# A diffusion block on one core: the state space's parameters at the head of the program, the modulation's early pieces behind the state-space stage

## The chip, the cores and the metric

One core of one Trainium2 chip runs the whole program. The metric is the device time of one execution in microseconds; a kernel's figure is the median over its runs. Times from the profile are microseconds from the first instruction of one profiled execution.

## The reference, cut to what matters

The reference is one layer of a hybrid backbone over 1024 latent tokens and 256 context tokens, 1024 features wide, all in float32.

```python
mod_x = silu(c) @ w_mod + b_mod              # six vectors: shift1, scale1, gate1, shift2, scale2, gate2
mod_c = silu(c_ctx) @ w_mod + b_mod
px = modulate(rmsnorm(x, g_norm_mix), sh1, sc1) @ w_in      # x: 1024 tokens
pc = modulate(rmsnorm(ctx, g_norm_mix), ch1, cc1) @ w_in    # context: 256 tokens
conv_x, fnet_x, qkv_x, ssm_x = split_cols(px)
y_conv = conformer_conv(conv_x, ...)         # gate, 31 taps, layernorm, silu, 256x256
y_fnet = fourier_mix(fnet_x, ...)
y_na   = neighbourhood_attention(q, k, v, k_ctx, v_ctx, rpb)
y_ssm  = s5_bidirectional(ssm_x, ssm_c, a_re, a_im, log_dt, b, c, d, w_glu, ...)
out = group_rmsnorm(concat(...)) @ w_out + b_out
x_mid = x + gt1 * out
x = x_mid + gt2 * mlp(modulate(rmsnorm(x_mid), sh2, sc2))   # squared ReLU, 4096 wide
return rmsnorm(x, g_final)
```

The state space runs in both directions over the context and then over the latent tokens, with 16 groups of 16 channels and 64 states. Its parameters come from `log_dt`, `a_re` and `a_im` through an exponential, a sine and a cosine, and powers of the result up to the ninth.

## The kernel before, in words

Data lies with features on the 128 partitions and tokens along the free axis. Latent tokens are worked on in two halves of 512 (`hf`). The products with `w_in` are done by tiles of 128 output features; each float32 operand is split into a high and a low part, so that a tile takes three matmuls for each of eight feature chunks.

The stages that the change touches, in program order:

- The **head**, lines 308 to 327. It loads x, and for each of eight chunks k the modulation weights for shift1 and scale1 (`load_wm`, two pieces of 512 KB), runs a small product with the conditioning vectors (`gemv`), sets `gsc`, and norms chunk k of both halves (`norm_x`: `nt` on VectorE, the high part on ScalarE, the low part `xl` on VectorE). Three weight tiles of `w_in` (12 and 13 for the state space, 8 for the keys) are loaded and split, with the low part `wlo` on GpSimd.
- The **x tiles** for these three, both halves (line 403 and on), 24 matmuls each, all recorded at line 364.
- **`mods(n)`**, line 335: n steps of the rest of the modulation. The first 16 of 32 pieces (gate1 and shift2) are done here, each a load of 512 KB (`wmB`, line 340), sixteen small matmuls (line 344), an eviction, and a pair of matmuls of the piece before (line 349). After each eight pieces VectorE sets `mod` (line 351). The other 16 are done in the attention.
- The **context**: eight loads (line 401), sum of squares, norm, and the context's part of tiles 12, 13 and 8. The results for the state space go to a tensor in memory, `us_d`.
- The state space's **parameters**, lines 440 to 581: about 60 small GpSimd operations, some 40 on VectorE, two sines on ScalarE, and the loads of `log_dt`, `bnat` and `cnat`.
- The **state-space blocks**: eight blocks of two groups. `ssm_setup(b)` builds the block's matrices on GpSimd and VectorE (`ca`, line 624, is the last GpSimd operation of it), with matmuls `pk` and transposes; `ssm_tables(b)` makes sine and cosine tables; `ssm_main(b)` reads `us_d` into `U`, multiplies, rotates (`ro`, from line 692), scans and writes `ys_d`. Setup and tables are called one block ahead.
- Then the tiles of `w_in` 9, 4 and 5, the values (`w_v`), `conv_in(0)` (two tiles whose product is `cv`, line 787), the GLU of the state space, the Fourier mixing, `conv_in(1)`, the queries, and the taps of the convolution on VectorE (line 1020). The attention follows, with an order of TensorE written by hand.

Up to the attention the order on each engine is not the program's: a planner takes, at each step of a modelled time, the ready operation that stands first in the program, and so fixes one in-order queue for each engine and for SP, which issues the loads. `tc.issue_after(ins)` makes what a block issues on the engine of `ins` stand behind `ins` in that queue. Tiles come from rings by tag: `wraw`, with three buffers, holds half of each `wm` pair, every `wmB` piece and every raw tile of `w_in` and `w_v`.

Of the kernel before, what the change touches and what calls it, by code (L numbers as in the profile page):

```python
# [8 lines left out]
F32 = mybir.dt.float32  # L9
# [8 lines left out]
P = 128  # L18
# [31 lines left out]
def body(tc, A, out, dbg=None):  # L50
# [256 lines left out]

    load_x(0)
    SP.dma_start(ident, A["cst"][:, 0:P])
    for k in range(8):  # L310
# [88 lines left out]
    for k in range(8):  # L399
        ctt.append(xp.tile([P, TC], F32, name="ctt", tag="hc", bufs=16))  # L400
        SP.dma_start(ctt[k], A["ctxT"][:, k, :])
# [8 lines left out]
    mods(4)  # L410
# [22 lines left out]
    mods(5)  # L433

    sset = ExitStack()
    sp = open_pool("ssm", "right", stack=sset)
    tst = ExitStack()
    tp = open_pool("tiny", "right", stack=tst)

    def tn(name, pool=None):  # L440
        return (pool or tp).tile([P, 16], F32, name="t_" + name)

    E_ = G
    ldt = tn("ldt")
    for d in range(2):
        SP.dma_start(ldt[d * 64:(d + 1) * 64, :], ap(A["log_dt"], d * 16, [[0, 64], [1, 16]]))

    def expparts(x, pre):

        n, r, w, sc = tn(pre + "n"), tn(pre + "r"), tn(pre + "w"), tn(pre + "s")  # L450
        E_.tensor_scalar(n, x, 1.4426950408889634, MAGIC, ALU.mult, ALU.add)
        E_.tensor_scalar(n, n, MAGIC, 1.0, ALU.subtract, ALU.mult)
        E_.tensor_scalar(n, n, -126.0, 127.0, ALU.max, ALU.min)
        V.scalar_tensor_tensor(r, n, -0.693145751953125, x, ALU.mult, ALU.add)
        V.scalar_tensor_tensor(r, n, -1.42860682030941723e-6, r, ALU.mult, ALU.add)
        E_.tensor_scalar(w, r, 1.0 / 5040, 1.0, ALU.mult, ALU.mult)
        for c in (1 / 720, 1 / 120, 1 / 24, 1 / 6, 0.5, 1.0):
            V.scalar_tensor_tensor(w, w, c, r, ALU.add, ALU.mult)
        E_.tensor_scalar(n, n, 127.0, 8388608.0, ALU.add, ALU.mult)
        ni = tp.tile([P, 16], I32, name="t_" + pre + "i")  # L460
        V.tensor_copy(ni, n)
        V.tensor_copy(sc, ni.bitcast(F32))
        return sc, w

    def tt(o, a, b, op, eng=None):
        (eng or E_).tensor_tensor(o, a, b, op)
        return o

    are, aim = C("are", 0, 16), C("aim", 0, 16)
    sc, w = expparts(ldt, "d")  # L470
    dt = tn("dt")
    tt(dt, sc, w, ALU.mult)
    tt(dt, dt, sc, ALU.add)
    ar, tau = tn("ar"), tn("tau")
    tt(ar, are, dt, ALU.mult)
    tt(tau, aim, dt, ALU.mult)
    E_.tensor_scalar(tau, tau, 0.15915494309189535, 1.0, ALU.mult, ALU.mult)
    kk = tn("kk")

    def frac(x):  # L480
        E_.tensor_scalar(kk, x, MAGIC, MAGIC, ALU.add, ALU.subtract)
        tt(x, x, kk, ALU.subtract)

    frac(tau)
    sc, w = expparts(ar, "e")
    Em, Ee = tn("Em"), tn("Ee")
    tt(Em, sc, w, ALU.mult)
    tt(Ee, Em, sc, ALU.add)
    V.scalar_tensor_tensor(Em, sc, -1.0, Em, ALU.add, ALU.add)
    sn, s2, cm = tn("sn"), tn("s2"), tn("cm")  # L490
    S.activation(sn, tau, AF.Sin, scale=TWO_PI)
    S.activation(s2, tau, AF.Sin, scale=PI_)
    tt(cm, s2, s2, ALU.mult)
    E_.tensor_scalar(cm, cm, -2.0, 1.0, ALU.mult, ALU.mult)
    pw_r = tp.tile([P, 10, 16], F32, name="pw_r")
    pw_i = tp.tile([P, 10, 16], F32, name="pw_i")
    V.memset(pw_r[:, 0, :], 1.0)
    V.memset(pw_i[:, 0, :], 0.0)
    mr, mi = tn("mr"), tn("mi")
    tt(pw_i[:, 1, :], Ee, sn, ALU.mult)  # L500
    V.scalar_tensor_tensor(pw_r[:, 1, :], cm, 1.0, Ee, ALU.add, ALU.mult)
    V.scalar_tensor_tensor(mr, cm, 1.0, Em, ALU.add, ALU.mult)
    tt(mr, mr, cm, ALU.add)
    mi = pw_i[:, 1, :]
    zr, zi, iv, t0 = tn("zr"), tn("zi"), tn("iv"), tn("t0")
    tt(iv, are, are, ALU.mult)
    tt(t0, aim, aim, ALU.mult)
    tt(iv, iv, t0, ALU.add)
    V.reciprocal(iv, iv)
    tt(zr, mr, are, ALU.mult)  # L510
    tt(t0, mi, aim, ALU.mult)
    tt(zr, zr, t0, ALU.add)
    tt(zr, zr, iv, ALU.mult)
    tt(zi, mi, are, ALU.mult)
    tt(t0, mr, aim, ALU.mult)
    tt(zi, zi, t0, ALU.subtract)
    tt(zi, zi, iv, ALU.mult)

    def cmul(orr, oi, ar_, ai_, br_, bi_, shape, tg, eng, neg_i=False):

        def tmp_():
            if shape is None:
                return sp.tile([P, 2, 160], F32, name="cm", tag="ss", bufs=4).rearrange(
                    "p a b -> p (a b)")[:, :256].rearrange("p (a b) -> p a b", a=16)
            return tp.tile(shape, F32, name="cm", tag=tg, bufs=2)
# [43 lines left out]
    for i in range(2):  # L569
        SP.dma_start(bn[i], A["bnat"][:, i, :])  # L570
# [12 lines left out]
    GB = 2  # L583
# [1355 lines left out]
```

## Time and profile before

| | us |
|---|---|
| median of 3 runs | 1326.41 |
| lowest and highest run | 1323.22, 1332.71 |
| the profiled execution | 1320.52 |
| its span, first to last instruction | 1318.4 |
| TensorE busy | 1182.3 |
| VectorE busy | 1025.8 |
| GpSimd busy | 799.6 |
| ScalarE busy | 650.7 |

The busy times are sums over the whole span, and the stages have different limits. PE is TensorE's matmuls, PEld its weight loads, DVE VectorE, ACT ScalarE, POOL GpSimd, SP the queue that issues loads. The TensorE clock is granted at one of two levels, 1.2 and 2.4 GHz, and a row gives the mean over its stretch as a share of the higher one.

### The profile page before, as it was taken

The numbers are of one execution on the slowest core, as the hardware profiler recorded it, in microseconds if no ns is written. First come the engines' busy times: TensorE is split into PE (matmuls) and PEld (weight loads), VectorE is DVE, ScalarE is ACT, GpSimd is POOL, SyncE is SP. The second block draws the span as 40 slices with busy tenths as digits, with TensorE's granted clock in tenths as the row PEclk, the third lists the DMA queues.
The fourth block names the chain that finished last, engine by engine and source line by source line (L and its number), as shares of the span: only waits on it lengthen the run. The fifth ranks groups of instructions, "written<-read, shape, count | busy, mean of one in ns | idle before, by whom it ended". The sixth has DMA issues, their size and how long they took to land.

```text
span 1318.4 us, 18813 instructions
## 1 busy us (share of the span) xinstructions
PE 1182.3 (90%) x6252; PEld 961.2 (73%) x6252; DVE 1025.8 (78%) x1604; ACT 650.7 (49%) x1335; POOL 799.6 (61%) x1004
## 2 busy tenths in 40 slices
PE   5997888997847889999989999999999999999995
PEld 3775667876636777877778787777877777877775
DVE  4657898599997857669794678888889888788877
ACT  5344334223255646555654454555544555545565
POOL 2147786472556642123566588777877777777764
PEclk9988998998876999999999999999999999999998
DMA  9554341251173554233120111111120111111113
GB/s 347 177 173 147 107 128 54 95 182 40 40 226 95 155 159 112 98 97 112 48 73 33 40 65 57 32 50 55 65 64 33 49 57 56 64 35 46 56 41 128
DMA packets 75058, 121.75 MB, mean 92 GB/s; under 512 B 16977, under 2 KB 35154, under 8 KB 74962
## 3 DMA queue, kind: packets, MB, share of 16 engines
q1 hardware_dynamic: 62802, 113.22, 26.6%
q10 hardware_dynamic: 12160, 7.34, 1.8%
q8 instruction: 49, 0.80, 0.3%
q14 instruction: 47, 0.39, 0.1%
HBM read 106.66 MB, written 13.88 MB: 91 GB/s over the span
## 4 chain that ended last, share of the span: by engine, by line
PE 52%; DVE 27%; ACT 5%; POOL 3%; DMA 3%; issue 3%; SPq 1%; ACTq 0%; DVEq 0%; POOLq 0%
PE fa L1477 11%; PE qa L1477 6%; PE qb L1477 6%; PE fb L1477 5%; DVE cacc L1020 3%; DVE tl L1493 3%; PE fc L1477 2%; PE p_t L1275 2%; PE mm L1102 2%; DVE fl L1493 2%; PE mm L364 2%; PE mm L1477 2%; DVE X L1498 1%; PE p_t L1263 1%; PE f L1477 1%
## 5 line engine op out<-in xcount | busy, mean ns | idle before, releaser
L1461 POOL TENSOR_TENSOR w2l<-w2r,w2h 128x128 fp32r<-128x128 f32 (+1 forms) x232 | 176.8, 763 | 68.8 <-ACT w2h L1460 61.1
L1498 DVE SCALAR_TENSOR_TENSOR X<-fa,gt2c,X 128x512 f32<-128x512 f32 x216 | 159.4, 745 | 13.9 <-PE fa L1477 13.9
L1460 ACT ACTIVATE w2h<-w2r 128x128 fp32r<-128x128 f32 (+1 forms) x232 | 86.1, 388 | 142.7 <-POOL w2r L1711 78.1
L235 POOL TENSOR_TENSOR wlo<-wraw,whi 128x1024 fp32r<-128x1024 f32 x30 | 74.3, 2479 | 124.0 <-ACT whi L233 118.2
L1461 POOL TENSOR_TENSOR w2l<-w1r,w2h 128x256 fp32r<-128x256 f32 x136 | 108.9, 817 | 61.2 <-ACT w2h L1460 34.4
L1498 DVE SCALAR_TENSOR_TENSOR X<-fb,gt2c,X 128x512 f32<-128x512 f32 x108 | 80.5, 745 | 36.5 <-PE fb L1477 36.0
L1461 POOL TENSOR_TENSOR w2l<-ws,w2h 128x256 fp32r<-128x256 f32 x84 | 67.9, 815 | 41.4 <-ACT w2h L1460 41.4
L1020 DVE SCALAR_TENSOR_TENSOR cacc<-cv,wdw,cacc 128x512 f32<-128x512 f32 x92 | 85.1, 971 | 0.4
L1477 PE MATMUL fa<-th,w2h 128*128 128x512 f32 x156 | 63.2, 405 | 19.7 <-DVE X L1498 19.7
L364 PE MATMUL mm<-xh,whi 128*128 128x512 f32 x192 | 77.1, 418 | 3.6 <-ACT xh L218 2.7
L364 PE MATMUL mm<-xl,whi 128*128 128x512 f32 x192 | 78.9, 411 | 0.5 <-DVE xl L220 0.5
L1460 ACT ACTIVATE w2h<-w1r 128x256 fp32r<-128x256 f32 x136 | 54.1, 410 | 48.7 <-DVE w1r L1614 19.1
L364 PE MATMUL mm<-xh,wlo 128*128 128x512 f32 x192 | 77.8, 407 | 0.0
L1477 PE MATMUL qa<-cb,w2h 128*128 128x512 f32 x224 | 70.6, 396 | 0.7 <-ACT ft L1629 0.7
L1493 DVE TENSOR_TENSOR fl<-ft,fh 128x512 fp32r<-128x512 f32 x64 | 56.1, 893 | 11.9 <-ACT fh L1492 11.3
L1477 PE MATMUL fa<-th,w2l 128*128 128x512 f32 x156 | 61.4, 394 | 0.8 <-POOL w2l L1461 0.8
L1477 PE MATMUL fa<-tl,w2h 128*128 128x512 f32 x156 | 61.5, 394 | 0.0
L1018 POOL TENSOR_TENSOR pacc<-pacc,ptmp 128x512 f32<-128x512 f32 x24 | 41.0, 1708 | 25.4 <-ACT ptmp L1017 25.4
L1460 ACT ACTIVATE w2h<-ws 128x256 fp32r<-128x256 f32 x84 | 33.2, 411 | 41.4 <-DVE ws L1610 20.7
L1477 PEld LDWEIGHTS fa<-th,w2h 128*128 128x128 f32 x156 | 29.3, 188 | 31.0 <-DVE X L1498 25.2
L1477 PEld LDWEIGHTS qa<-cb,w2h 128*128 128x128 f32 x224 | 42.0, 188 | 11.3 <-ACT ft L1629 1.1
L1484 ACT ACTIVATE ft<-ft,colf 128x512 f32<-128x512 f32 x42 | 30.5, 727 | 35.4 <-DVE ft L1632 35.4
(787 smaller groups left out, 3893.0 us busy)
## 6 DMA issues: line engine op xcount, KB each, us to landing
w2r<-in_w_ff SPq DMA_DIRECT2D x68, 256.0 KB
wmB<-in_wmodB SPq DMA_DIRECT2D x32, 512.0 KB
w1r<-in_w_ff SPq DMA_DIRECT2D x64, 256.0 KB
wm<-in_wmodA SPq DMA_DIRECT2D x16, 512.0 KB
wraw<-in_w_in SPq DMA_DIRECT2D x12, 512.0 KB
x<-in_xT SPq DMA_DIRECT2D x8, 512.0 KB
wraw<-in_w_out SPq DMA_DIRECT2D x8, 512.0 KB
kr<-k_d SPq DMA_DIRECT2D x16, 256.0 KB
```

The costliest lines, as they stand in the source:

```text
L235: (lo_eng or G).tensor_tensor(lo, raw, hi.bitcast(F32), ALU.subtract)
L364: PE.matmul(o, a_[:, k, :], b_[hf][k], start=k == 0 and i == 0, stop=k == 7 and i == 2)
L1018: G.tensor_tensor(pacc, pacc, t, ALU.add)
L1020: V.scalar_tensor_tensor(acc, x(k), w(k), acc, ALU.mult, ALU.add)
L1102: PE.matmul(o, a_[:, 2 * kk + c, :], b_, start=c == 0 and i == 0, stop=c == 1 and i == 2)
L1275: PE.matmul(po[:, j * 64:j * 64 + 64], ptt[:, i * P:(i + 1) * P], rv, start=i == 0, stop=i == 4, skip_group_check=True)
L1460: S.activation(hi, a, AF.Copy)
L1461: G.tensor_tensor(lo, a, hi.bitcast(F32), ALU.subtract)
L1477: PE.matmul(o, a_[:, i, :], m_, start=start and j == 0, stop=stop and j == 2, skip_group_check=True)
L1484: S.activation(t, t if src is None else src, AF.Relu, bias=CF("b_ff1", f))
L1493: V.tensor_tensor(lo, t, hi.bitcast(F32), ALU.subtract)
L1498: return V.scalar_tensor_tensor(x, o, gt2(k), x, ALU.mult, ALU.add).ins
```

## The change

The parameter code becomes two functions. `ssm_loads` issues its five loads, and is called before the first modulation weights; `ssm_params` does the arithmetic, and is called in step 1 of the head's loop. The first block's `ssm_setup` is called in step 4. The pools of the state space are opened ahead of the head; two of the three `cx` tiles with their zeroing are made there, the third in the pool that is opened where the parameters were. The calls `mods(4)` and `mods(5)` around the context go away. Behind the state-space stage stand `mods(1)` and four times `mods(2)`, then one step after `conv_in(0)`, one before `conv_in(1)`, four between the queries and two ahead of the taps. What is between the state space and the values stands in a block of `issue_after` the last context load.

```diff
+    PR = {}
+    def ssm_loads():
+        ldt = tn("ldt")
+        for d in range(2):
+            SP.dma_start(ldt[d * 64:(d + 1) * 64, :], ap(A["log_dt"], d * 16, [[0, 64], [1, 16]]))
...
+        for i in range(2):
+            SP.dma_start(bn[i], A["bnat"][:, i, :])
+        SP.dma_start(cn, A["cnat"])
+        PR["loads"] = ldt, bn, cn
+
+    def ssm_params():
...
-    cxs = [sp.tile([P, 2, GB, 272], F32, name=f"cx{i}") for i in range(3)]
-    for t in cxs:
-        G.memset(t, 0.0)
+    cxs = []
+
+    def new_cx(pool):
+        cxs.append(pool.tile([P, 2, GB, 272], F32, name=f"cx{len(cxs)}"))
+        G.memset(cxs[-1], 0.0)
...
+    new_cx(sp)
+    new_cx(sp)
+    ready = []
+    load_x(0)
+    SP.dma_start(ident, A["cst"][:, 0:P])
+    ssm_loads()
+    for k in range(8):
+        wm = load_wm(k)
...
+        norm_x(0, pbs[0], k)
+        if k == 1:
+            ssm_params()
+        if k == 4:
+            ready.append(ssm_setup(0))
...
+        ctx_in = SP.dma_start(ctt[k], A["ctxT"][:, k, :]).ins
...
     gvp = ps_tile("gv", "gvp")
-    mods(4)
     ch, cl = modnorm(xp, sumsq(xp, ctt, TC), ctt, TC,
...
     k_ctx(8)
-    mods(5)
...
-    ready = [ssm_setup(0) + ssm_tables(0)]
+    rho, th_h, th_l = PR["rho"], PR["th_h"], PR["th_l"]
+    new_cx(sp2)
+    ready[0] += ssm_tables(0)
     for b in range(NB_):
...
-    mods(1)
-    cw[9] = load_w(A["w_in"][9])
-    for hf in range(2):
-        ev_k(9, hf, x_tile(cw[9], hf))
-    k_ctx(9)
-    mods(0)
-    for ti in (4, 5):
-        w = load_w(A["w_in"][ti])
+    with tc.issue_after(ctx_in):
+        mods(1)
+        cw[9] = load_w(A["w_in"][9])
         for hf in range(2):
-            ev_u(ti, hf, x_tile(w, hf))
-            mods(2)
+            ev_k(9, hf, x_tile(cw[9], hf))
+        k_ctx(9)
+        for ti in (4, 5):
+            w = load_w(A["w_in"][ti])
+            for hf in range(2):
+                ev_u(ti, hf, x_tile(w, hf))
+                mods(2)
...
     conv_in(0)
+    mods(1)
...
+    mods(1)
     conv_in(1)
...
-    mods(1)
+    mods(2)
     for _ in tap_steps(0, 0):
```

## Rows read from the trace of the kernel before

**Rows 1.** Busy time by stretch: us, engines (instructions), TensorE clock, DMA share, GB/s.

```profile
0.00:31.00 31.00, 15.30 (x80) 10.29 (x81) 13.08 (x30) 16.68 (x27) 7.03 (x10) 1.00 0.96 353
31.00:75.20 44.20, 43.85 (x258) 32.17 (x256) 27.15 (x53) 16.24 (x29) 5.85 (x8) 1.00 0.48 159
75.20:97.00 21.80, 18.84 (x199) 15.13 (x199) 14.30 (x60) 11.05 (x29) 13.66 (x54) 0.77 0.67 215
97.00:128.00 31.00, 23.52 (x160) 18.37 (x159) 21.95 (x35) 11.78 (x27) 24.41 (x37) 0.83 0.55 164
128.00:257.00 129.00, 117.75 (x854) 95.83 (x854) 104.89 (x165) 50.12 (x108) 89.52 (x99) 0.96 0.29 91
257.00:389.00 132.00, 106.34 (x469) 86.25 (x467) 119.79 (x149) 46.82 (x72) 70.83 (x42) 0.88 0.36 115
...
79.00:104.00 25.00, 21.42 (x220) 17.79 (x212) 18.28 (x67) 9.66 (x24) 20.66 (x70) 0.81 0.67 213
```

**Rows 2.** VectorE by line, 257 to 389 us: busy, mean ns, idle before.

```profile
L1020 DVE SCALAR_TENSOR_TENSOR cacc<-cv,wdw,cacc 128x512 f32<-128x512 f32 x89 | 82.5, 974 | 0.4
...
L787 DVE SCALAR_TENSOR_TENSOR cv<-cth,mm 128x512 f32<-128x512 f32 x4 | 2.7, 677 | 5.7 <-PE mm L364 5.7
```

**Rows 3.** TensorE's waits, 75 to 257 us: us in total, times, longest.

```profile
PE pg L344 <- DMA wmB<-in_wmodB: 5.0, 1, 5.0
PE gvp L344 <- DVE mod L351: 1.8, 1, 1.8
```

**Rows 4.** The chain of waits, 90 to 260 us: start, us, what.

```profile
104.18 6.68 DMA wmB<-in_wmodB
```

**Rows 5.** SP's queue in order of time: start, us, what it issued.

```profile
50.56 11.09 SPq L340 DMA_DIRECT2D wmB<-in_wmodB  x3
61.75 4.75 SPq L401 DMA_DIRECT2D ctt<-in_ctxT  x8
...
100.69 2.58 SPq L679 DMA_DIRECT2D U<-us_d  x4
```

**Rows 6.** GpSimd and VectorE in order of time: start, us, what, [idle before].

```profile
70.47 0.20 POOL L451 TENSOR_SCALAR t_dn<-t_ldt 128x16 f32<-128x16 f32 x1 [29.93 <-DMA t_ldt<-in_log_dt]
...
114.18 0.95 POOL L624 TENSOR_TENSOR ca<-ca,cs 128x320 f32<-128x320 f32 x1
...
86.01 1.26 DVE L215 SCALAR_TENSOR_TENSOR nt<-ctt,gsc,pb 128x256 f32<-128x256 f32 x3
```

**Rows 7.** DMA issues of the first 130 us, by tile.

```profile
bn<-in_bnat SPq DMA_DIRECT2D x2, 128.0 KB
cn<-in_cnat SPq DMA_DIRECT2D x1, 256.0 KB
```

**Rows 8.** GpSimd and VectorE in time; then one group by line, 79 to 128 us.

```profile
146.22 2.46 POOL L235 TENSOR_TENSOR wlo<-wraw,whi 128x1024 fp32r<-128x1024 f32 x1
...
146.48 2.55 DVE L666 TENSOR_TENSOR ph<-p,ph 128x318 f32<-128x318 f32 x1
...
120.08 0.49 DVE L666 TENSOR_TENSOR ph<-p,ph 128x318 f32<-128x318 f32 x1
...
L220 DVE SCALAR_TENSOR_TENSOR cl<-nt,mod,ch 128x256 fp32r<-128x256 f32 x8 | 3.9, 488 | 0.2 <-ACT ch L218 0.2
```

**Rows 9.** TensorE in order of time: pieces of the modulation.

```profile
79.44 0.59 PE L349 MATMUL gvp<-cst,gv_rows 128*128 128x2 f32 x2
...
99.72 0.28 PE L349 MATMUL gvp<-cst,gv_rows 128*128 128x2 f32 x2
99.93 0.65 PE L344 MATMUL pg<-wmB,sT 128*32 128x128 f32 x16
...
111.00 1.08 PE L344 MATMUL pg<-wmB,sT 128*32 128x128 f32 x16 [4.97 <-DMA wmB<-in_wmodB]
```

**Rows 10.** The blocks' first rotation by tile: ns, first and last start.

```profile
L692 DVE TENSOR_TENSOR ro<-Ss,cst__1211 x1: 500/500/500, 130.9 to 130.9; 128x318 f32<-128x318 f32 x1
...
L692 DVE TENSOR_TENSOR ro<-Ss,cst__1946 x1: 2642/2642/2642, 243.8 to 243.8; 128x318 f32<-128x318 f32 x1
```

More of the change, by code (lines that the diff above doesn't have):

```diff
@@ L306, in add_rstd, with tn @@
         S.copy(pbs[hf], rstd_bc(p1, pbs[hf], H, 0, (mm_tile, at_tile)[hf], NS))
+    sset = ExitStack()
+    sp = open_pool("ssm", "right", stack=sset)
+    tst = ExitStack()
+    tp = open_pool("tiny", "right", stack=tst)
+    GB = 2
+    NB_ = 16 // GB
+    fl = lambda t: t.rearrange("p g q -> p (g q)")
+    v4 = lambda t: t.rearrange("p g (s m) -> p g s m", m=16)
+    b3 = lambda t: t.rearrange("p (g m) -> p g m", g=16)
+    PR = {}
+    def tn(name, pool=None):
+        return (pool or tp).tile([P, 16], F32, name="t_" + name)
@@ new lines, in ssm_loads @@
+    def ssm_loads():
+        ldt = tn("ldt")
+        for d in range(2):
+            SP.dma_start(ldt[d * 64:(d + 1) * 64, :], ap(A["log_dt"], d * 16, [[0, 64], [1, 16]]))
+        bn = [sp.tile([P, 2, 160], F32, name="bn", tag="ss", bufs=4).rearrange("p a b -> p (a b)")[:, :256]
+              for _ in range(2)]
+        cn = sp.tile([P, 2, 256], F32, name="cn")
+        for i in range(2):
+            SP.dma_start(bn[i], A["bnat"][:, i, :])
+        SP.dma_start(cn, A["cnat"])
+        PR["loads"] = ldt, bn, cn
@@ L400, in body @@
         ctt.append(xp.tile([P, TC], F32, name="ctt", tag="hc", bufs=16))
-        SP.dma_start(ctt[k], A["ctxT"][:, k, :])
+        ctx_in = SP.dma_start(ctt[k], A["ctxT"][:, k, :]).ins
     for hf in range(2):
@@ L432, in body @@
     k_ctx(8)
-    mods(5)
[L435 to L525, printed above, removed]
-        t1, t2 = tmp_(), tmp_()
-        eng.tensor_tensor(t1, ai_, bi_, ALU.mult)
-        eng.tensor_tensor(orr, ar_, br_, ALU.mult)
-        eng.tensor_tensor(orr, orr, t1, ALU.subtract)
-        eng.tensor_tensor(t2, ai_, br_, ALU.mult)
-        eng.tensor_tensor(oi, ar_, bi_, ALU.mult)
-        if neg_i:
-            V.scalar_tensor_tensor(oi, oi, -1.0, t2, ALU.mult, ALU.subtract)
-        else:
-            eng.tensor_tensor(oi, oi, t2, ALU.add)
@@ L550, in body @@
-    pb_i = sp.tile([P, 8, 16], F32, name="pb_i")
-    for dst, src in ((pa_r, pw_r), (pa_i, pw_i)):
-        V.tensor_copy(dst[0:64], src[0:64])
-        V.tensor_copy(dst[64:128], src[64:128, ::-1, :])
-    for dst, src in ((pb_r, pw_r), (pb_i, pw_i)):
-        V.tensor_copy(dst[0:64], src[0:64, 0:8, :])
-        V.tensor_copy(dst[64:128], src[64:128, 7::-1, :])
-    rho, th_h, th_l = [tn(n, sp) for n in ("rho", "thh", "thl")]
-    th8 = tn("th8")
-    tt(rho, Ee, Ee, ALU.mult)
-    tt(rho, rho, rho, ALU.mult)
@@ L561, in body @@
-    tt(rho, rho, rho, ALU.mult)
-    E_.tensor_scalar(th8, tau, 8.0, 1.0, ALU.mult, ALU.mult)
-    frac(th8)
-    E_.tensor_scalar(th_h, th8, 1536.0, 1536.0, ALU.add, ALU.subtract)
-    tt(th_l, th8, th_h, ALU.subtract)
-    bn = [sp.tile([P, 2, 160], F32, name="bn", tag="ss", bufs=4).rearrange("p a b -> p (a b)")[:, :256]
-          for _ in range(2)]
-    cn = sp.tile([P, 2, 256], F32, name="cn")
-    for i in range(2):
-        SP.dma_start(bn[i], A["bnat"][:, i, :])
-    SP.dma_start(cn, A["cnat"])
@@ L584, in body @@
-    NB_ = 16 // GB
-    fl = lambda t: t.rearrange("p g q -> p (g q)")
-    v4 = lambda t: t.rearrange("p g (s m) -> p g s m", m=16)
     sp2 = open_pool("ssm2", "right", stack=sset)
```

245 lines of the change are left out of this document (173 added, 72 removed).

## The prediction, on record before the run

> **What bounds the kernel now.** I read the table by stretches first. From 31 to 75 us TensorE is busy 43.85 of 44.2 us: the six x tiles with eight gemv steps between them. From 75.2 to 128 us it idles 2.96 + 7.48 us and its granted clock is 0.77 and 0.83, a mix of the 2.4 and the 1.2 GHz level. From 128 to 257 us it is busy 117.75 of 129 us, ahead of VectorE (104.89) and GpSimd (89.52). From 257 to 389 us VectorE is busy 119.79 of 132 us [rows 1]. So the stage that ends last changes hands at 257 us. What the hand-over waits for is in VectorE's groups by line: 89 of the conv's taps fall behind 257 us and take 82.5 us, and ahead of them line 787, which makes their input, waits 5.7 us for the matmuls of `conv_in(0)` [rows 2]. TensorE's pace up to the last tile of `conv_in(0)` therefore sets when VectorE's saturated tail starts, and from 389 us the attention, whose TensorE order is written by hand, follows that tail.
>
> Then I asked why TensorE idles between 75 and 128 us. Its waits name the modulation: 5.0 us for one 512 KB piece, 1.8 us for VectorE's `mod` behind another [rows 3]; the chain of waits has the same transfer with 6.68 us [rows 4]. SP's queue shows what those pieces displace: it stands 11.09 us in three issues of `wmB` from 50.56 us, and only then, at 61.75 us, issues the eight context loads; the state space's first input `U` is asked for at 100.69 us [rows 5]. The parameters start late too: GpSimd's first of them waits 29.93 us for `log_dt`, queued behind the context, and the first block's `ca` comes at 114.18 us. The context's first norm is at 86.01 us, though TensorE had finished the x tiles at 75.2 us [rows 6].
>
> **The change part by part.** The parts are summed to the end of `conv_in(0)`, now 257 us, and the tail follows that one to one.
>
> (a) *Five loads move ahead of the first modulation weights* on SP's queue: twice 128 KB, 256 KB and two of a few KB [rows 7]. At the 353 GB/s of the first 31 us [rows 1] that is 0.5 MB / 353 = 1.5 us, if the first gemv waits for all of it. The bytes were moved within that same stretch before, so the other end is 0. I take +1, above the middle, as the transfers are 96% busy there.
>
> (b) *The parameters and the first `ssm_setup` run under the x tiles.* Their cover is TensorE's 43.85 us. From 79 to 104 us, which holds nearly the whole parameter chain, VectorE is busy 18.28 us [rows 1], of which the context's sixteen norm operations are 3.9 us for eight [rows 8] and about as much for the other eight: 10.5 us are left, and the first setup adds some 2 (an estimate: four operations of about 0.5 us, as the unhindered 318-column one in rows 8). VectorE has 44.2 - 27.15 = 17 us free in the head; GpSimd takes 20.66 us in that stretch and has 38 free [rows 1]. So 0, with the chain's latency (70.47 to 114.18 us [rows 6], 44 us) covered if it starts before 30 us. If the cover goes, each microsecond by which the setup's matmuls stand unready in TensorE's queue goes straight into the end, since the x tiles are queued behind them. The setup's own matmuls leave one side of the sum and join the other.
>
> (c) *The early modulation pieces leave the way of the context.* All sixteen loads stand behind the last context load in SP's queue (`issue_after`), so the context loads are free to go about 11 us earlier [rows 5]. Statistics and norms then run under the x tiles, and the context's matmuls can follow at 75 us. What can go is the idle time, 10.4 us at most [rows 1]; at least nothing, if other waits take its place. I take -9: the named waits in rows 3 belong to `mods` by their tile names, and some small wait will stand in their place. What is late next is the first block's `U`, a round trip through memory; under it lie `w_in[9]`'s tiles, as now.
>
> (d) *The clock.* At the full level the busy time of 75 to 128 us would be shorter by 18.84 x 0.23 + 23.52 x 0.17 = 8.3 us [rows 1]. The low level came with the idle gaps of (c). Ends 0 and -8.3; I take -5, nearer to the far end, because the stretches on both sides (no gaps over a few us) show 1.00 and 0.96.
>
> (e) *Seven of sixteen pieces go behind `conv_in(0)`.* By program order nine calls of `mods` stand ahead of it, the rest behind. A piece is sixteen matmuls and the pair for the one before it: 0.65 + 0.28 us at the high clock, 1.08 + 0.59 us at the low one [rows 9]. Seven are 6.5 to 11.7 us, and the planner may pull some forward again into gaps, which makes it 0 to -11.7; I take -5. In the tail they lie in TensorE's 132 - 106.34 = 26 us of idle time [rows 1], so they cost nothing there; the gate that needs the first eight is not used before the attention.
>
> (f) *The state-space blocks* start earlier, by up to 30 us by (b) and (c). They now take (243.8 - 130.9) / 7 = 16.1 us each [rows 10] and end with `conv_in(0)`. I count no gain for that: TensorE is the busiest engine there and has the same tiles to do. Two of the three `cx` tiles' memsets stay at the start, the third falls in GpSimd's idle time: 0.
>
> Sum: +1 - 9 - 5 - 5 = **-18 us**. Against the profiled execution's own 1320.52 us (span 1318.4) that is 1302.5; it lies 5.9 us under the median of the runs shown, so against that median 1326.41 - 18 = **1308 us**.
>
> One rule speaks against (b). When GpSimd runs a 2.46 us `wlo`, VectorE's two-input `ph` takes 2.55 us and ends with it, against 0.49 us alone; but the eight `cl` operations, also with two inputs, ran at 488 ns beside the small parameter operations [rows 8]. The Trainium skill (SBUF — State Buffer, "SBUF: two separate sides") says that GpSimd and a VectorE operation with two SBUF inputs hold a port pair exclusively, and that the loser blocks for the whole instruction. By that rule the norms of the head would stall behind every parameter operation; the trace bears it out for large tiles only, and it is rival C below.
>
> **The rivals.**
> *A: the waits move with the pieces.* The sixteen loads still take ring slots of three and still stand in an in-order TensorE queue; if the planner places them as before, only later, (c) and (d) return between 128 and 257 us. Left is +1 - 5 = -4: 1322 us. For it: the wait of 5.0 us was one that the planner had not foreseen. Against it: the DMA share is 0.29 from 128 to 257 us and was 0.55 to 0.67 where that wait stood [rows 1].
>
> *B: slower.* The pieces share the ring of three `wraw` buffers with `w_in[9]`, `w_in[4]`, `w_in[5]`, the two `w_v` and `conv_in`'s four loads, and all of them are now wanted in the same stretch. If seven pieces each hold TensorE for the 5.0 us that one held it [rows 3], that is 35 us: -18 + 35 = +17, 1343 us. It decides from the fourth such wait on (18 / 5.0 = 3.6). For it: nine of the sixteen were through before the first block, and now compete with its tiles. Against it: only one in sixteen waited like that, at the higher DMA load.
>
> *C: the head stretches.* The first setup has ten GpSimd operations of up to 0.95 us (`ca` in rows 6). If each blocks a norm for its length, the head, in which TensorE has 0.35 us to spare, grows by up to 9.5 us: -8.5, 1318 us. Against it are the `cl` operations of rows 8.
>
> *D: the change gives more*, because the state-space stage, done 30 us earlier, leaves VectorE and GpSimd free for the GLU and the taps. With the far ends of (c), (d) and (e) and nothing for (a): -10.4 - 8.3 - 11.7 = -30, 1296 us.
>
> **How the numbers follow.** About 1% (13 us) is what a measurement of this kernel can tell from no change. Forecast 0.48 and D 0.08, both faster by over 1%; A 0.26 and C 0.07, both within; B 0.11. That is 0.56, 0.33 and 0.11. The bounds of the unknown terms run from -30 to +1.5, 1296 to 1328 us; the median of three runs adds a little at the low side. I give **1294 to 1328 us**, which leaves out B and what lies under D.
>
> **What would show it.** (a) the first gemv matmul 0 to 1.5 us later than now. (b) the last x tile still at 75 to 78 us, the first block's `pk` before it. (c) context loads issued near 50 us, the context's first norm under the x tiles, no `wmB` wait of over 2 us on TensorE before 128 us. (d) a clock above 0.95 from 75 to 128 us. (e) `conv_in(0)` done at 235 to 242 us, some `wmB` matmuls at line 344's place behind it, and taps that start with it. The forecast is wrong if the x tiles end after 80 us, if TensorE's idle time from 75 us to the end of `conv_in(0)` stays above 20 us, or if VectorE's tail starts earlier and the first scores do not.

## The result, and the profile after the change

The changed kernel takes **1338.26 us** (median of 20 runs, 1328.74 to 1344.80) against 1328.87 us for the kernel before beside it (20 runs, 1321.23 to 1336.22): ratio 1.007, 95% interval 1.0049 to 1.009. Forecast was 1308 us, 18 us less; measured are 9.4 us more. That is under the 1% of the forecast, but the interval leaves no doubt about the sign, and the time lies above the stated range.

The profiled execution took 1337.78 us (span 1336.0), close to its median; that of before lies some 8 us under the median of these 20 runs. The two traces are therefore 17.6 us apart where the medians are 9.4 apart, and about 8 us of what follows belong to the one run of before, not to the change. The stretches after the change, with the columns of [rows 1]:

```profile
0.00:31.00 31.00, 11.61 (x62) 7.74 (x62) 17.82 (x52) 18.04 (x29) 19.93 (x60) 1.00 0.95 341
31.00:75.20 44.20, 37.69 (x210) 26.34 (x210) 31.36 (x50) 13.80 (x24) 32.37 (x49) 1.00 0.39 124
75.20:97.00 21.80, 15.47 (x94) 11.78 (x94) 14.66 (x32) 13.25 (x28) 0.66 (x1) 0.96 0.54 169
97.00:128.00 31.00, 24.09 (x168) 19.00 (x169) 19.43 (x51) 13.16 (x31) 15.99 (x19) 0.86 0.35 90
128.00:257.00 129.00, 118.61 (x874) 95.73 (x873) 90.73 (x157) 44.73 (x101) 78.30 (x87) 0.97 0.34 106
257.00:389.00 132.00, 112.83 (x564) 90.59 (x562) 115.02 (x150) 49.97 (x78) 52.91 (x33) 0.91 0.38 122
```

TensorE idles more in the head: 31 - 11.61 = 19.4 us before 31 us and 6.5 us from there to 75.2 us, against 15.7 and 0.35 [rows 1]. TensorE's granted clock of 75 to 97 us did rise, from 0.77 to 0.96 (1.00 is the level of 2.4 GHz, 0.50 that of 1.2). But from 257 us VectorE, the engine that was to be the bound there, is busy 4.8 us less than before.

Stretches of fixed time hide what has moved, so I laid both traces out by events: each time is the start of the first or last instruction of a tile or line, and the idle columns give the length from the event above to this one minus TensorE's busy time in it.

| event (us) | before | after | TensorE idle up to it, before | after |
|---|---|---|---|---|
| first `kt` eviction (x tiles end) | 74.9 | 90.1 | 16.1 | 26.6 |
| first norm of the context | 86.0 | 104.0 | 3.0 | 10.4 |
| first rotation of the blocks | 130.9 | 130.8 | 7.5 | 2.2 |
| last rotation | 243.8 | 234.8 | 11.2 | 10.3 |
| first `cv` (input of the taps) | 262.8 | 273.3 | 0.0 | 0.0 |
| first score | 385.5 | 397.3 | 24.7 | 24.4 |
| last score | 553.3 | 570.9 | 26.4 | 27.3 |
| end of the span | 1318.4 | 1336.0 | | |

From the last score to the end both take 765.1 us: everything is decided before it. Of the 17.6 us, 10.5 are there at the first `cv`, 1.3 come up to the first score and 5.8 in the attention. By another cut they are 12.3 us more of idle time and 5.3 us more of busy time for about as many matmuls. Of these 5.3 us, 4.9 lie in the attention, where the granted clock was 0.85 instead of 0.89; from the first to the last score it took 163.9 to 177.6 us over all the traces of this case, so single traces do not show whether the change has a part in those 5.8 us.

**The head.** GpSimd, VectorE and TensorE, each in order of time (start, us, what, [idle before]):

```profile
19.73 2.35 POOL L235 TENSOR_TENSOR wlo<-wraw,whi 128x1024 fp32r<-128x1024 f32 x1
...
25.30 0.74 POOL L360 TENSOR_TENSOR t_rho<-t_rho 128x16 f32<-128x16 f32 x1
...
26.98 0.21 POOL L360 TENSOR_TENSOR t_rho<-t_rho 128x16 f32<-128x16 f32 x1
...
37.97 2.34 POOL L235 TENSOR_TENSOR wlo<-wraw,whi 128x1024 fp32r<-128x1024 f32 x1
...
19.80 2.30 DVE L549 TENSOR_SCALAR gsc<-mod,cols 128x2 f32<-128x2 f32 x1
...
33.81 0.38 DVE L449 COPY pb_r<-pw_r 64x128 f32<-64x128 f32 x1 [4.21 <-POOL pw_r L424]
...
36.48 3.92 DVE L446 COPY pa_r<-pw_r 64x160 f32<-64x160 f32 x1 [0.19 <-POOL pw_r L424]
40.42 0.24 DVE L447 COPY pa_r<-pw_r 64x160 f32<-64x160 f32 x1
...
41.68 2.98 DVE L215 SCALAR_TENSOR_TENSOR nt<-x,gsc,acc 128x512 f32<-128x512 f32 x3
...
43.62 1.22 PE L601 MATMUL mm<-xh,whi 128*128 128x512 f32 x2 [4.86 <-DVE nt L215]
```

VectorE's queue is worked off in order. The copies that lay out the powers stand in it ahead of the norms of the head: one waits 4.21 us for GpSimd, one takes 3.92 us beside GpSimd's work (its twin takes 0.24), and the three norms behind them start at 41.68 us (32.52 us before). TensorE waits 4.86 us for them. The lateness starts sooner: `gsc`, which took 0.23 us there before, takes 2.30 us beside a `wlo`, and the first x-tile matmul comes at 23.79 us instead of 21.04. And it is more than waiting: the x tiles end 15.2 us later with 10.5 us more of idle time, and the other 4.7 us are busy time. The first setup's matmuls are 1.6 us of them; of the rest, about 3 us, most come from x-tile matmuls that start every 0.43 us until 51.7 us and every 0.23 us behind it, a pace that they had from 34.6 us before. The granted clock of these stretches is 1.00 in both traces, so it does not show why.

**SP's queue** (start, us, what it issued) answers to [rows 5]:

```profile
33.44 24.63 SPq L299 DMA_DIRECT2D wm<-in_wmodA  x8
66.91 0.80 SPq L527 DMA_DIRECT2D kb<-kt__584  x2
68.34 1.42 SPq L528 DMA_DIRECT2D tz<-kb  x2
69.80 8.83 SPq L638 DMA_DIRECT2D ctt<-in_ctxT  x8
```

The context loads go out at 69.80 us, 8 us later than the 61.75 of before. The last modulation weights ahead of them are issued by 58.07 us (48.24 before), as the head itself is late. And the first setup has a round trip through memory of its own, `kb` and `tz`, and that stands in the queue ahead of them until the setup's last evictions. TensorE's waits from 75 to 274 us (us in total, times, longest) are other ones than in [rows 3], and no shorter:

```profile
PE pa L183 <- DVE acc L210: 6.0, 1, 6.0
PE pb L195 <- DVE rf L174: 4.4, 1, 4.4
```

Both belong to the context's statistics. The modulation's wait is gone; the statistics' came in its place.

**Ahead of the attention**, TensorE in order of time:

```profile
373.29 1.16 PE L195 MATMUL pb<-ident,rc 128*128 128x128 f32 x8 [1.91 <-DVE rc L188]
382.99 1.08 PE L581 MATMUL pg<-wmB,sT 128*32 128x128 f32 x16 [8.54 <-DVE yf L259]
...
389.71 1.08 PE L581 MATMUL pg<-wmB,sT 128*32 128x128 f32 x16 [0.69 <-DMA wmB<-in_wmodB]
393.89 1.08 PE L581 MATMUL gvp<-wmB,sT 128*32 128x128 f32 x16 [3.10 <-DMA wmB<-in_wmodB]
...
397.35 0.67 PE L1270 MATMUL p_s<-kh,qq 128*128 128x384 f32 x1
```

A late piece of the modulation waits 8.54 us for VectorE's `yf`, since pieces and group norms take turns at the PSUM buffer `gn`; five pieces, three of them shown, then stand in TensorE's queue ahead of the first score.

VectorE's taps by line from 257 to 389 us, which answer to [rows 2] (91 of them there, 89 before):

```profile
L1046 DVE SCALAR_TENSOR_TENSOR cacc<-cv,wdw,cacc 128x512 f32<-128x512 f32 x91 | 79.8, 916 | 0.7
```

The blocks' first rotation by tile (ns, first and last start), the first and the last block, which answer to [rows 10]:

```profile
L714 DVE TENSOR_TENSOR ro<-Ss,cst__1089 x1: 492/492/492, 130.8 to 130.8; 128x318 f32<-128x318 f32 x1
...
L714 DVE TENSOR_TENSOR ro<-Ss,cst__1824 x1: 491/491/491, 234.8 to 234.8; 128x318 f32<-128x318 f32 x1
```

### The profile page after: what moved, and what is told of

Read it like the earlier page. It is cut to its first block, busy times and chain, and to the rows that moved or that the text cites. A ratio compares the mean times of both kernels' runs of the same rounds, so it can differ in the third digit from the quotient of the medians.

```text
span 1336.0 us, 18810 instructions
## 1 busy us (share of the span) xinstructions
PE 1187.4 (89%) x6252; PEld 963.0 (72%) x6252; DVE 1014.2 (76%) x1604; ACT 652.6 (49%) x1339; POOL 792.2 (59%) x1004
## 3 DMA queue, kind: packets, MB, share of 16 engines
q1 hardware_dynamic: 62802, 113.22, 27.3%
## 4 chain that ended last, share of the span: by engine, by line
PE 52%; DVE 27%; DMA 6%; ACT 6%; issue 4%; POOL 4%; SPq 1%; ACTq 0%; DVEq 0%; POOLq 0%
PE fa L1503 10%; PE qa L1503 6%; PE qb L1503 5%; PE fb L1503 5%; PE mm L601 4%; DVE cacc L1046 3%; DVE tl L1519 3%; PE mm L1128 2%; PE fc L1503 2%; PE p_t L1301 2%; DMA wraw<-in_w_out 2%; DVE fl L1519 2%; PE mm L1503 2%; DVE X L1524 1%; DVE Ss L723 1%
## 5 line engine op out<-in xcount | busy, mean ns | idle before, releaser
L1046 DVE SCALAR_TENSOR_TENSOR cacc<-cv,wdw,cacc 128x512 f32<-128x512 f32 x92 | 80.5, 915 | 0.7
L1044 POOL TENSOR_TENSOR pacc<-pacc,ptmp 128x512 f32<-128x512 f32 x24 | 36.5, 1521 | 30.2 <-ACT ptmp L1043 30.2
L233 ACT ACTIVATE whi<-wraw 128x1024 fp32r<-128x1024 f32 x30 | 31.7, 1057 | 45.0 <-DMA wraw<-in_w_out 22.2
L601 PEld LDWEIGHTS mm<-xh,whi 128*128 128x128 f32 x192 | 37.4, 196 | 22.3 <-ACT xh L218 11.4
```

Of the source, the lines that this page charges most:

```text
L233: S.activation(hi, raw, AF.Copy)
L601: PE.matmul(o, a_[:, k, :], b_[hf][k], start=k == 0 and i == 0, stop=k == 7 and i == 2)
L1044: G.tensor_tensor(pacc, pacc, t, ALU.add)
L1046: V.scalar_tensor_tensor(acc, x(k), w(k), acc, ALU.mult, ALU.add)
```

## The experiments

Each was timed beside the kernel before (1324 to 1325 us there); a ratio is to it, with its 95% interval. The changed kernel is at 1.007. A trace is of one run of a kernel, which can lie several us off its median; so where traces are compared, the events in them count and not their ends.

**1. The change in parts.** Four kernels, from the changed one unless said otherwise.

```diff
 # e1: the first setup again behind the context
-        if k == 4:
-            ready.append(ssm_setup(0))
...
-    ready[0] += ssm_tables(0)
+    ready.append(ssm_setup(0) + ssm_tables(0))
 # e4: e1, and the parameters' calls written behind the head's loop
-        if k == 1:
-            ssm_params()
...
+    ssm_params()
 # e2: before, with the pieces moved as in the change; e3: after, with the pieces at their old places
```

> The changed kernel with the first block's setup called behind the context again; the parameters stay in step 1 of the head's loop. Head theory (the parameter operations on VectorE and GpSimd stand ahead of the norms, so the x tiles end at 89 us in place of 75): little comes back, the x tiles still end at 84 to 89 us, and the time is 2 to 6 us under the changed kernel, +0.3 to +0.6% against before. Queue theory (the setup's kb and tz transfers stand in SP's queue ahead of the context loads, 66.9 to 69.8 us, and TensorE then idles until 103 us for the context's norm): the context loads go at 58 to 61 us, the context's first norm comes 8 to 10 us earlier, and the time is 8 us or more under the changed kernel, level with before. Tail theory (late modulation pieces hold the weight ring): no change from the changed kernel, +0.7%.

> The changed kernel with the parameter arithmetic called behind the head's loop (its loads stay at the start) and the first setup behind the context, so that the norms stand before both in the planner's choice. Head theory: VectorE's copies no longer stand ahead of norms, the x tiles end at 75 to 79 us and the kernel is level with before or faster by up to 1%. Queue theory: like the run with the setup alone moved back. Tail theory: +0.7% as the changed kernel.

> The kernel before with the modulation's early pieces moved behind the state-space stage as in the change, and nothing else. The sum of the prediction without its head part gives -9 -5 -5 = -19 us, -1.4%. Head theory: the x tiles end at 75 us, the context loads go near 50 us, and the kernel is faster than before by 0.5 to 1.4%. Queue theory: the same, as no setup stands in the queue. Tail theory: +0.3 to +0.7% against before, with waits for weights between 385 and 405 us as in the changed kernel.

> The changed kernel with the modulation's early pieces back at their old places: only the parameters and the first setup are moved. Head theory: x tiles end at 84 to 89 us and the kernel is 0.7% or more slower than before. Queue theory: the same sign, but the context's late norm (100 us or later) carries it. Tail theory: level with before or faster, within 0.3%.

Measured: e1 1331.34 us, 1.0048 (1.0026 to 1.0071); e4 1333.86 us, 1.0066 (1.0043 to 1.009); e2 1342.12 us, **1.013** (1.0102 to 1.0159); e3 1326.99 us, **1.0023** (1.0002 to 1.0043). Neither part gains, and the two don't add up: the pieces' move costs 1.3% by itself, and 0.5% with the head moved. In e3 the x tiles end at 90.6 us as in the changed kernel, in e1 at 87.2, in e4 at 88.2. Where the calls are written in the program hardly matters: in e4 the planner pulls the parameters forward again (the first at 10.57 us), and in e1, as in e4, most of the setup too. In e1, from GpSimd's and SP's queues:

```profile
40.73 0.80 POOL L505 TENSOR_TENSOR ca<-pa_r,cn 128x320 f32<-128x320 f32 x1 [0.43 <-DVE pa_r L447]
...
57.58 13.34 SPq L636 DMA_DIRECT2D ctt<-in_ctxT  x8
```

That is the setup's `ca`, at the time that it has in the changed kernel (40.74 us). Only the setup's matmuls, its round trip through memory and what follows them went behind the context. So the 2.9 us that e1 takes off the head are the price of these, and the head without the setup was not run. The context loads go 12 us earlier in e1 than in the changed kernel, and still the norm (101.2 us) stands 14.0 us behind the end of the x tiles, as it does there (13.9).

In e2 the first `cv` comes where it was before (263.2 us), and 19.0 of the 22.5 us by which its last score is later lie between there and the first score (404.9 us). Over all its runs the mean granted clock is 0.944, and 0.954 in the kernel before beside it.

**2. Lateness or the first nine pieces.** Only the calls of `mods` differ.

```diff
 # e5: after, all sixteen ahead of conv_in(0), no later calls;  e7: the same on e2
-                mods(2)
+                mods(4)
...
 # e6: before, the first nine as they were, the last seven behind conv_in(0)
-    mods(1)
...
-            mods(2)
...
     conv_in(0)
+    mods(1)
...
```

> The changed kernel with all sixteen modulation pieces ahead of conv_in(0) (four at each of the four u tiles instead of two), none behind it; the parameters and first setup stay at the head. Theory 'late ring' (the late pieces hold the w_out loads back and stand in TensorE's queue where attention begins): the first w_out load goes back from 390 us to about 260, the first scores come 4 to 10 us sooner than in the changed kernel, and the time falls to that of the kernel with the head move alone, 1325 to 1330 us. Theory 'early loss' (what costs is that TensorE lacks the pieces while it waits for the context norm and the pieces then fall into the state-space blocks): time stays at 1335 to 1342 us.

> The kernel before with only the last seven modulation pieces taken from the u tiles and put behind conv_in(0), where the changed kernel has them; the first nine stay where they were and the head is as before. Theory 'late ring': slower by 0.8 to 1.3% (1336 to 1342 us), nearly all that the pieces' move cost alone, with the first w_out load at 380 us or later. Theory 'early loss': within 0.3% of before, 1322 to 1329 us, since the nine pieces in the context norm's wait are untouched.

> The kernel before with the first nine pieces moved behind the state-space stage as in the change, but all sixteen done ahead of conv_in(0). Theory 'late ring': 1325 to 1331 us, at most 0.4% above before. Theory 'early loss': 1336 to 1344 us, as with the pieces' move whole (1342).

Measured: e5 1330.03 us, 1.0044 (1.0021 to 1.0068); e6 1321.27 us, **0.9992** (0.9961 to 1.0024); e7 1329.56 us, 1.0022 (0.9996 to 1.0048). e7 is e2 with the last seven pieces ahead of `conv_in(0)`: that takes back nearly all of the 1.3%, and the first score comes at 388.4 us instead of 404.9. From the changed kernel to e5 the same move takes back 0.26%, with the first score at 387.8 instead of 397.3. So the late pieces cost 1.1%, 0.3% or, from the kernel before to e6, nothing, by the order that they fall into; my theory of the "late ring" foretold a loss for e6 and fell, in that form. In e6 lateness did both things at once: the first `cv` comes at 257.1 us, 5.7 sooner than before, just the 5 us of my term (e), and the first score at 388.0, 2.5 later. What the pieces give ahead of `conv_in(0)` they take back ahead of the attention. In e6, the tile `cv` (ns, first and last start):

```profile
L785 DVE SCALAR_TENSOR_TENSOR cv<-cth,mm x4: 673/676/689, 257.1 to 327.3; 128x512 f32<-128x512 f32 x4
```

and TensorE in order of time shows the same row of pieces ahead of the scores as in the changed kernel:

```profile
376.03 1.08 PE L344 MATMUL pg<-wmB,sT 128*32 128x128 f32 x16 [1.59 <-DVE yf L259]
...
387.96 0.67 PE L1244 MATMUL p_s<-kh,qq 128*128 128x384 f32 x1
```

**3. The context's loads alone**, on the kernel before:

```diff
-    mods(4)
+    with tc.issue_after(ctx_in):
+        mods(4)
```

> The kernel before with one edit: the loads of the first four modulation pieces are held until the last of the eight context loads has been issued; no piece changes its place on TensorE. My predicted term for this was 9 us less up to the first rotation. Theory 'the context norm waits for its loads': first norm 8 to 11 us sooner than 86 us, first rotation sooner, 1315 to 1320 us. Theory 'the norm waits for its statistics in the queues of ScalarE and VectorE, and the blocks for the parameters': loads about 11 us sooner, first norm at most 3 us sooner, first rotation at 129 to 133 us, time within 0.3% of before.

Measured: 1330.27 us, 1.0039 (1.001 to 1.0068). SP's queue and the first context norm in this kernel:

```profile
51.56 8.91 SPq L401 DMA_DIRECT2D ctt<-in_ctxT  x8
60.56 19.59 SPq L340 DMA_DIRECT2D wmB<-in_wmodB  x3
80.25 1.71 SPq L447 DMA_DIRECT2D t_ldt<-in_log_dt  x2
...
88.56 1.26 DVE L215 SCALAR_TENSOR_TENSOR nt<-ctt,gsc,pb 128x256 f32<-128x256 f32 x3 [2.10 <-PE pb L195]
```

The loads go out 10 us earlier than before and the norm starts 2.6 us later. It does not wait for its loads; it follows the end of the x tiles (78.1 us here, 10.5 us ahead of it). The time of e8 says less: behind the held pieces the load of `log_dt` went out at 80.25 us instead of 66.76, the parameters started 15 us later than before (85.92 against 70.47 us), and the first rotation came at 145.8 us instead of 130.9.

**4. The copies, and the least of the change.**

```diff
 # e9: the changed kernel; e10: e3 and e1 together with it
-            V.tensor_copy(dst[0:64], src[0:64])     # and the seven like it
+            G.tensor_copy(dst[0:64], src[0:64])
```

> The changed kernel with the eight copies that lay out the state space's powers (pa and pb) given to GpSimd instead of VectorE; nothing else. In the changed kernel they stand in VectorE's queue ahead of the second half's norms, wait 4.2 us for GpSimd and take 7.1 us, and the three norms start at 41.7 us instead of 32.5. Theory 'the copies in VectorE's queue stretch the head': the norms start at 33 to 36 us, the x tiles end 5 to 9 us sooner than 90 us, and the time falls by 4 to 8 us against the changed kernel (ratio to before 1.001 to 1.004). Rival 'the first setup and the port stretch it': x tiles end within 3 us of 90 us and the time stays within 3 us of the changed kernel (1.005 to 1.009).

> The least of the change: the parameters alone at the head, with the copies on GpSimd; the first setup behind the context, and all sixteen pieces where they were before the change. Theory 'each of the three moves costs by itself and the early parameters are worth something without them': first rotation at 118 to 126 us instead of 131, time 1314 to 1322 us, ratio 0.993 to 0.998. Rival 'the first rotation waits for the context tiles and not for the parameters': first rotation at 128 to 134 us, ratio 0.998 to 1.003.

Measured: e9 1333.01 us, 1.0049 (1.0023 to 1.0075); e10 1329.68 us, 1.0024 (1.0003 to 1.0045). In e9 the three norms start at 37.2 us instead of 41.7, but the x tiles end at 88.2 us, only 2 sooner: the copies were the largest single wait, and behind them the next stood ready. In e10 they end at 83.0 us, still 8 late, and the first rotation does come earlier, at 125.2 us, though the time is no shorter. VectorE's first context norms in e10 in order of time, then the first rotation by tile:

```profile
98.15 1.26 DVE L215 SCALAR_TENSOR_TENSOR nt<-ctt,gsc,pb 128x256 f32<-128x256 f32 x3 [1.81 <-PE pb L195]
```

```profile
L714 DVE TENSOR_TENSOR ro<-Ss,cst__1211 x1: 1031/1031/1031, 125.2 to 125.2; 128x318 f32<-128x318 f32 x1
```

This showed what the runs have in common. **From the context's first norm to the first rotation** it is 26.6 to 30.0 us in all eleven kernels that have the parameters at the head, and 44.9 to 57.2 us in all seven that don't. The parameters had been late by 15 us or more, as I had read it; but each kernel that moved them got its context norm 12 to 20 us later.

**5. The price of the pieces.** Fifteen of sixteen are left out (no load, no gemv, no eviction; the first one's rows stand in for all).

```diff
-            if i < MODS:
+            if i == 0:
                 wm = wts.tile([P, 8, P], F32, name="wmB", tag="wraw", bufs=3)
...
```

> The kernel before without the loads, gemvs and evictions of fifteen of the sixteen modulation pieces (the first piece's rows stand in for all); the small matmuls that gather them stay. What the pieces cost where they stood is the difference to before. Theory 'they filled TensorE's wait for the context norm and cost next to nothing there': 1316 to 1325 us. Rival 'they cost their matmul time, 16 times about 2 us, nearly whole': 1292 to 1305 us.

> The changed kernel without the same fifteen pieces; what is left is the head's move. Theory 'the pieces cost more behind the state space than ahead of it': it gains 4 to 10 us more against the changed kernel than the kernel before gains by the same cut, and comes within 3 us of the kernel before without pieces. Rival 'the head's move is what costs': 8 to 12 us above the kernel before without pieces.

Measured: the kernel before without pieces takes 1332.51 us, **1.0045** (1.0025 to 1.0066); the changed one 1321.49 us, **0.9971** (0.9946 to 0.9996). The kernel before is slower with less work. Without pieces the head's move gains 0.74% (0.9971 / 1.0045), about 10 us; with them at their old places (e3) it costs 0.23%. But 0.45% of the 0.74 are what the kernel before lost by the cut: with fifteen pieces less to do, the changed one is only 0.29% under the whole kernel before. VectorE and TensorE from 257 to 389 us, first before, then after, both without pieces (columns as above):

```profile
257.00:389.00 132.00, 104.05 (x435) 81.60 (x434) 129.42 (x155) 42.64 (x66) 66.42 (x44) 0.83 0.30 95
```

```profile
257.00:389.00 132.00, 102.18 (x465) 83.36 (x463) 131.27 (x160) 53.56 (x81) 68.57 (x43) 0.87 0.37 119
```

In the kernel before without pieces TensorE's granted clock is 0.83 there instead of 0.88, and 0.938 over the span instead of 0.958 (0.944 against 0.953 over all runs); up to the last score it is busy 470.6 us, 6.2 more than with the pieces. Whether the missing pieces lowered the clock, or the order that the planner wrote without them did, these runs don't separate.

**6. The shared PSUM buffer.**

```diff
 # e13: after;  e16: before
-                pg = gvp[:, 0:P] if i % 2 else ps_tile("gn", "pg", P)
+                pg = gvp[:, (i % 2) * P:(i % 2 + 1) * P]
 # e14: after, the seven late pieces together
     conv_in(0)
-    mods(1)
+    mods(8)
...
 # e15: e5, e1, e9 and e13 in one
```

> The changed kernel with one edit: every modulation piece writes its rows into one of two quarters of the PSUM tile gvp, where until now every second piece took the buffer gn, which the group norms use as well. In the changed kernel a late piece waits 8.5 us for that buffer and six pieces then stand ahead of the first score. Theory 'shared buffer': no such wait, the pieces run where TensorE has gaps, first score 4 to 9 us sooner than 397 us, and 3 to 6 us less than the changed kernel (ratio to before 1.002 to 1.005). Theory 'queue and ring': the pieces still wait for their weights and stand at the end, first score within 3 us of 397 us, ratio 1.005 to 1.009.

> The changed kernel with the seven late pieces all right behind conv_in(0) instead of spread from there to the second q tile. Theory 'queue and ring': first w_out load at 280 to 330 us instead of 390, no piece ahead of the first score, first score 5 to 10 us sooner than 397 us, ratio 1.003 to 1.006, as with all pieces ahead of conv_in(0). Theory 'shared buffer': the pieces wait for the group norm's buffer all the same and hold TensorE during the state space's group norms; first score within 4 us of 397 us, ratio 1.005 to 1.010.

> The changed kernel with what single runs showed to be cheaper: the powers' copies on GpSimd, the first setup behind the context, all sixteen pieces ahead of conv_in(0) and in their own PSUM quarters. If the three losses add up (0.2% each for copies, setup and lateness) it comes to 1322 to 1327 us, ratio 0.998 to 1.002; if each only shifts the wait to the next in line, to 1328 to 1333 us, ratio 1.003 to 1.006.

> The control: the kernel before with the same edit of the pieces' PSUM tile. All its pieces are done by 160 us, before the first group norm, so both theories expect no difference: ratio 0.998 to 1.002.

Measured: e13 1327.83 us, **1.0025** (1.0008 to 1.0043); e14 1334.55 us, 1.0063 (1.0047 to 1.0079); e15 1327.68 us, 1.0032 (1.0013 to 1.005); e16 1335.03 us, **1.0069** (1.0052 to 1.0087). In e13 the wait for `yf` is gone, the last piece is done by 381 us, and the first score waits for VectorE instead:

```profile
375.62 0.64 PE L581 MATMUL gvp<-wmB,sT 128*32 128x128 f32 x16
...
378.85 0.65 PE L581 MATMUL gvp<-wmB,sT 128*32 128x128 f32 x16 [2.27 <-ACT gv_rows L594]
...
385.45 0.69 PE L1270 MATMUL p_s<-kh,qq 128*128 128x384 f32 x1 [4.51 <-DVE qq L996]
```

That is the first score at 385.5 us, as before the change, and two thirds of the loss back. In e14 the first `w_out` load goes out at 305 us (389.6 in the changed kernel) and the first score comes 5.8 us sooner, at 391.5, but the attention takes 177.6 us instead of 173.6 and the time is the same within the intervals: no gain from the ring of raw weights is shown. e15, with four of the edits together, is no better than e13 alone: what they take off does not add up. The control e16 surprised both theories. There the early pieces wait for one another's evictions,

```profile
PE gvp L344 <- ACT gv_rows L357: 7.4, 5, 3.3
```

and the first `cv` comes at 277.4 us instead of 262.8, by an edit that touches nothing near it: 10.4 of the 14.6 us are TensorE work that now stands behind the last rotation (29.4 us instead of 19.0). So a buffer of their own took a wait away from pieces among group norms, and the same edit cost 0.7% where the pieces stand in a row; most of what moved there is the order of the tiles, which the planner wrote anew. A difference under 0.7% is by itself no measure of a mechanism, e13's 0.45% and those of 0.2 and 0.3% above included; what I rest on are events in the traces that moved where an edit said that they would. No kernel that does the whole work beat the kernel before by more than its interval.

## Why the prediction was wrong, point by point

**(a), the five loads, +1.** The first gemv matmul starts at 14.42 us, before at 12.18: 2.2 us later, more than the 1.5 that I allowed, but because the matmuls of the statistics went ahead of it (12.62 us). Both gemv halves and the statistics were through at 16.4 us instead of 16.1, so the term itself was small, and not what decided.

**(b), "So 0": the step that failed first.** I compared VectorE's free time in the head, 17 us, with the 12.5 us to be added, and GpSimd's 38 with 21. Both did fit: from 31 to 75.2 us VectorE went from 27.15 to 31.36 us and GpSimd from 5.85 to 32.37, though GpSimd's addition came out nearly twice as large as my 21 (26.5 us there and 12.9 ahead of 31 us). But free time is not cover on an in-order queue. The parameter chain changes between GpSimd and VectorE many times, and whatever waits for GpSimd holds the norms behind it. The x tiles end 15.2 us later and TensorE idles 10.5 us more. That each microsecond lost there would go "straight into the end" did not hold either: in e3 the x tiles end 15.7 us later than before, the first `cv` comes 14.5 us later, the first score 5.8, and the time is 0.23% longer. Of the 15.2 us, e1 takes off 3, e9 (the copies) 2, and e10, with both and the pieces at their old places, 7. The other 8 stay open: they hold the rest of the chain and the setup's operations on GpSimd and VectorE, which stood in the head in each of these runs.

Rival C had the place and foretold up to 9.5 us; its mechanism was only part. GpSimd's 128x16 operations did not slow VectorE's two-input ones: it is GpSimd whose `t_rho` took 0.74 us there and 0.21 alone. The setup's larger ones did: the three norms beside them took 2.98 us, and 2.08 before; how much that makes in all no run shows, as the setup's operations stayed in the head. The copy of 3.92 us, which ended with the last of three GpSimd operations in a row (36.59 to 40.31 us), looks like such a blocking. The Trainium skill (SBUF — State Buffer, "SBUF: two separate sides") has the pair of ports held for a whole instruction and the loser blocked; both rows agree with that, and the first says that the loser can well be GpSimd. That one copy is held over three operations in a row goes beyond that section.

**(c), -9: failed twice.** The loads did not go earlier, since I left the DMAs of the moved setup out of SP's queue (66.91 and 68.34 us); without these they go at 57.58 us (e1), still not near 50, as the head is late. And they would not have helped: in e1 and e8 they go 12 and 10 us earlier than in the kernels that these were made from, and the norm keeps its place behind the x tiles. [rows 6] show the norm at 86.01 us, 11 us behind the x tiles' end; I took the loads at 61.75 us for the cause because SP's queue held them up, and did not ask what else the norm waits for. In every trace here the norm starts 10 to 17 us behind the x tiles' end: statistics on ScalarE and VectorE, a matmul, the root's refinement on VectorE, another matmul. The -9 measured +1: the idle time from the x tiles' end to `conv_in(0)`'s first output is 23.0 us after and 21.7 before, which is what I had said would prove me wrong.

**(d), -5.** The clock of 75 to 97 us rose to 0.96 and that of 97 to 128 us to 0.86. Right in sign, and by luck: up to 90.1 us the x tiles now fill that stretch (1.00), and in the wait that follows, to the context norm at 104.0 us, the clock was 0.69, as low as in the same wait before (0.64). The idle time that was to go, and the low clock with it, is still there.

**(e), -5 and "cost nothing" in the tail.** The -5 is borne out where it could be seen alone: -5.7 in e6. The cover was wrong again, and of the same kind: 26 us of idle TensorE, but those are for the most part waits for VectorE, its group norms above all, and the pieces share a PSUM buffer with them and come out of the wait in one row ahead of the first score. In e6 that gave back 8.2 us, in the changed kernel own buffers bring the first score 11.8 us forward and regain about 6 us (e13 against 1.007).

**(f), 0.** The blocks took 104.0 us instead of 112.9, VectorE having 83.3 us to do in them instead of 94.7 (four `ca` there instead of six). But x and context tiles that used to be done under them now stand behind: 38.5 us of TensorE work, with no gap, between the last rotation and the first `cv`, instead of 19.0.

**"The tail follows that one to one", the base of the sum: not so.** From the first `cv` to the first score it is 122.7 us before and 107.1 (e5) to 141.7 us (e2) in the other traces. In e16 the first `cv` comes 14.6 us later and the first score 5.7; in e10 the one comes 7.8 us later and the other 3.9 us sooner; in e6 it is the other way round. So even a right sum up to `conv_in(0)` would not have given the time.

**The rivals.** B had the sign, not the mechanism: after 75 us no piece waited over 3.1 us for its weights. What is shown, as events, is that the head's stretch moved the x tiles' end, that the pieces' new company held up the first score, and that the parameters' gain (18 us between context norm and first rotation) was real and was eaten by the context norm, 18.0 us later. In time, the pieces' move costs 1.3% by itself; the 0.23% of the head's move by itself are too little to tell from an order written anew. Left open: how much of the head's 15.2 us the setup costs; why the late pieces cost so much more in e2 than with the head moved; and why the kernel before is slower with fifteen pieces less. The second and the third come with a lower clock (0.944 over all runs in both, 0.953 and 0.954 in the kernel before). That the pieces fill TensorE's waits and so keep its clock up would fit the third; it is argued, not shown.

## What to carry to other kernels

An engine's idle share is no cover for work that is put into its in-order queue: walk the queue, and ask of each instruction that you add what it waits for and who stands behind it, its DMAs included. Leaving work out did not always save time here, and where a call stands in the program did not settle where the planner put it; so price a move by leaving the work out at both places, and look in the trace whether an edit moved what it says. A sum to one event gives the time only if what follows keeps its length; check that. When a step becomes ready earlier, ask which of its other inputs comes last; here the move took 18 us out of the stretch between the context norm and the first rotation, and brought the norm itself 18 us later.

## What I had not expected of the hardware

The parameters' sine between two roots gives ScalarE two more table loads in the head, of 1.28 us each (before, one stood there and the sine's came at 83.16 us). The third lies in a wait, since the root behind it starts at 31.56 us, when TensorE's sums are there:

```profile
10.99 1.28 ACT L186 ACT_TABLE_LOAD   x1
16.81 1.28 ACT L385 ACT_TABLE_LOAD   x1
28.86 1.28 ACT L186 ACT_TABLE_LOAD   x1
```

A GpSimd operation of 128x16 elements took up to three and a half times as long beside VectorE's 512-column ones (0.74 against 0.21 us), while those kept their 0.74 us; and a VectorE copy of 64x160 elements took 3.92 us beside three GpSimd operations in a row, the last of them a `wlo` of 128x1024, and 0.24 us alone.
